# A third buffer for shuffled numerators, products 28 chunks behind the scores, and seven block products in the output projection

## Chip, cores and metric

The kernel runs on one core of one Trainium2 chip. The metric is device time in microseconds (us) of one execution. The profiled execution lists five engines: PE (TensorE: matmuls, with PEld for its weight loads), DVE (VectorE), ACT (ScalarE), POOL (GpSimd) and SP (SyncE, which here issues every DMA).

## What is computed

One layer of a diffusion backbone: RMS norm with adaLN, one input projection, two branches, one output projection. Cut to what the change touches (S = 2048 tokens, 256 context tokens, D = 1024, 4 heads, value width 128):

```python
q, k, v = _mla_qkv(u, ...)                       # latent queries
k_all = jnp.concatenate([kc, k], axis=2)         # 256 + 2048 keys
v_all = jnp.concatenate([vc, v], axis=2)
s = jnp.einsum('bhqd,bhkd->bhqk', qblk, k).astype(jnp.float32) * scale
p = jax.nn.softmax(s, axis=-1)
attn = jnp.einsum('bhqk,bhkd->bhqd', p.astype(v.dtype), v)
br_a = jax.nn.silu(gate_a) * attn
br_p = jax.nn.silu(gate_p) * _multiscale_pool(pool_in, w_pool, pool_scale)
y = jnp.concatenate([br_a, br_p], axis=-1) @ w_out[l]
x_new = x + gate[:, None, :] * y
```

Everything is float32. The kernel gets float32 accuracy out of cheaper matmuls by splitting each operand in a high part (ACT copies it to a narrower type) and a low part (the rest, by a subtraction on DVE or POOL), and makes three products: high x high, high x low, low x high.

## The kernel before

The stages are: loads and modulation (to about 100 us), the input projection and its features (`feat`, `tok`, `prod`, to about 515 us), attention (to 1124 us), output projection (to the end). The change lies in the last two.

**Attention.** There are 4 heads x 4 blocks of 512 queries. A block is two half-blocks p of 256 queries, so p runs from 0 to 31 (`NP` = 32); p is even for a block's first half and odd for its second. `scores(p, i)` (i = 0, 1: 128 queries each) makes the scores of 2304 keys in five pieces ("chunks": `CHUNKS`, four of 512 keys and one of 256), each of five matmuls (L772), the row maxima on DVE (L775), exponentials on ACT (L793) with their sums, and a 32x32 transpose on DVE (L796) into a buffer of `tbuf`. A half-block is thus ten chunks. When both i are done, `shuffle(p)` moves the 32x32 squares into place with 16 DMAs on SP (L811), from `tbuf[p % 2]` to `pbuf[p % 2]`: two shuffled buffers, both from the pool "W" (5 buffers). For the last half-block, p = 31, there is no shuffle: `pv_last` lets PE transpose.

`pv(p)` makes the products of probabilities and latent values. It has nine steps j2; for each, `halves(j2)` makes the high part on ACT (L853) and the low part on POOL (L855; on DVE for j2 = 4 and for some at the end), two steps ahead, into a tile of the pool "M" (6 buffers), and `pv_mm` makes six matmuls (L821) into the one bank "O" of a block. `norm(n)` takes a block's sums, inverts and transposes them, stores them to `rvd` (L879, L881), loads them back broadcast (`rb`, L884), loads the gate (`ga`, L886), and multiplies the two on POOL (L887). `latents(n)` splits bank O (ACT and DVE), and `finish(n)` multiplies by the value weights (three matmuls, L903) and by the gate on DVE (L905) and stores the block's branch to `brd` (L908). `finish` of a block comes at k == 2 in the products of the next.

**What sets the order.** `attn` yields after each chunk; `pv_all` is advanced so that its steps lie `LAG` = 22 chunks behind (L964: `while done < (gc - LAG) * 9 / PER`). This is the order in which the code is recorded; the framework's scheduler then sets each engine's order by simulated times, so the built order can differ. On each engine instructions run in that built order, so a waiting one holds up all behind it. `tc.issue_after(shuffle(p))` puts loads of keys (`load_k`) and of `w_out` (`load_wo`, for p in `WO_PF`) behind a shuffle on SP.

**End of attention and output.** When the scores are all recorded, about 20 steps of products remain: the last of p = 29, `pv_last` (p = 31) and `pv(30)`. Between them `out_weights` splits `w_out` in eight pieces at the steps in `WO_AT`. Then come eight pairs of 128-token tiles (t2): load of `brd` (1 MB), a split of 128x2048, and for each of 2 tiles x 2 halves of 512 columns, 8 x 3 matmuls (L1028) into a bank of "A" (5 banks); the last bank of the last pair is made in two halves of 256 columns. The result times the gate is made on DVE out of PSUM (L1049), plus x on POOL (L1052; on DVE for the last), and stored. For the first pair the matmuls are recorded by contraction steps, so that PE can start with those weights that are split first.

## Time and profile before

| | |
|---|---|
| times of 3 runs | 1288.63, 1289.4, 1295.37 us; median 1289.4 |
| profiled execution | 1288.46 us; its span (first to last instruction) 1286.7 us |
| mean granted TensorE clock | 0.984 of full speed |
| busy share: PE, PEld, DVE, ACT, POOL | 94%, 74%, 65%, 57%, 44% |
| output matmuls L1028 | 792 |
| score matmuls L772, product matmuls L821 | 1600, 1728 |

The profile's first part gives each engine's busy time; matmuls overlap, so a mean duration of one is longer than the distance between two. A row of the timeline is: start (us), duration (us), engine, line, operation, out<-in, shapes, and in brackets the idle time just before it and what ended it. A row that ends in x6 merges six instructions in a row.

### The profile page before, as it was taken

What the parts mean: (1) busy time and instruction counts of PE and PEld (TensorE: products, weight loads), DVE (VectorE), ACT (ScalarE), POOL (GpSimd) and SP (SyncE); (2) the same over time, 40 slices, a digit from 0 to 9 for tenths busy, and PEclk for the clock granted to TensorE, in tenths of its full rate; (3) what the DMA queues carried; (4) which work ended last, traced back from release to release, by engine and by line L of the source; (5) the groups of instructions that cost most, each with busy time, mean ns of one, the idle gap of its engine ahead of it and who ended that gap; (6) DMA issues with size and microseconds to landing.
All of it is one profiled execution on the core that took longest, in us unless ns stands there. A gap on an engine that the chain in (4) does not pass through costs nothing.

```text
span 1286.7 us, 22292 instructions
## 1 busy us (share of the span) xinstructions
PE 1212.8 (94%) x7805; PEld 954.5 (74%) x7805; DVE 831.1 (65%) x1595; ACT 738.5 (57%) x1780; POOL 562.1 (44%) x638
## 2 busy tenths in 40 slices
PE   6799999999999998988999989999899999899998
PEld 3698989989899998755566655666556667688887
DVE  4966654765666555677788887888778887631211
ACT  5575665655575654466777767777667777511000
POOL 3645313524344342025566645654656654332221
PEclk9799999999999999999999999999999999999999
DMA  9446952574446547367877787777777778563321
GB/s 304 149 122 138 228 137 66 130 198 136 94 108 153 113 126 196 90 150 172 199 188 181 182 203 188 182 176 196 185 176 183 179 191 236 194 238 135 115 98 49
DMA packets 208213, 208.66 MB, mean 162 GB/s; under 512 B 92339, under 2 KB 168420, under 8 KB 207974
## 3 DMA queue, kind: packets, MB, share of 16 engines
q1 hardware_dynamic: 208102, 207.25, 62.0%
q8 instruction: 61, 1.00, 0.3%
q14 instruction: 50, 0.41, 0.1%
HBM read 98.50 MB, written 35.56 MB: 104 GB/s over the span
## 4 chain that ended last, share of the span: by engine, by line
PE 70%; DMA 11%; DVE 5%; SPq 5%; ACT 4%; issue 2%; POOL 2%; ACTq 0%; DVEq 0%; POOLq 0%
PE pA L588 17%; PE pA L1028 14%; PE pA L772 14%; PE pO L821 9%; PE pA L244 6%; SPq L811 3%; PE pA L519 2%; POOL M L855 2%; DMA M<-in_w_in_dram 2%; DMA rvd<-rr 2%; ACT M L853 2%; PE pX L772 1%; DMA W<-W 1%; DVE W L796 1%; PE pA L494 1%
## 5 line engine op out<-in xcount | busy, mean ns | idle before, releaser
L855 POOL TENSOR_TENSOR M<-W,M 128x512 f16<-128x512 f32 x244 | 291.3, 1218 | 193.3 <-ACT M L853 193.2
L772 PE MATMUL pA<-B,M 128*128 128x512 f16 x1280 | 303.9, 381 | 7.0 <-ACT T L793 3.6
L588 PE MATMUL pA<-W,B 128*128 128x256 f32 x2304 | 307.3, 287 | 0.1
L588 PEld LDWEIGHTS pA<-W,B 128*128 128x128 f32 x2304 | 290.2, 192 | 3.5 <-issue 0.9
L772 PEld LDWEIGHTS <-M 128*128 128x128 f16 x1600 | 156.4, 98 | 145.6 <-issue 7.3
L821 PE MATMUL pO<-M,B 128*128 128x256 f16 x1728 | 222.1, 276 | 21.2 <-POOL M L855 20.3
L793 ACT ACTIVATE T<-pA,nm,gm 128x512 f32<-128x512 f32 x248 | 189.6, 775 | 62.7 <-DVE nm L781 62.7
L821 PEld LDWEIGHTS <-B 128*128 128x128 f16 x1728 | 168.9, 99 | 71.6 <-issue 31.6
L796 DVE STREAM_TRANSPOSE W<-T 128x512 f32<-128x512 f32 x310 | 197.6, 647 | 25.2 <-ACT T L793 14.3
L853 ACT ACTIVATE M<-W 128x512 f16<-128x512 f32 x279 | 164.7, 632 | 84.3 <-PE pO L821 65.2
L775 DVE TENSOR_REDUCE mx<-pA 128x1 f32<-128x512 f32 x256 | 173.3, 680 | 37.8 <-PE pA L772 36.3
L1028 PE MATMUL pA<-W,B 128*128 128x512 f32 (+1 forms) x792 | 178.7, 386 | 4.8 <-ACT B L96 4.8
L1028 PEld LDWEIGHTS pA<-W,B 128*128 128x128 f32 x792 | 146.0, 189 | 34.2 <-ACT B L96 5.1
L1052 POOL TENSOR_TENSOR M<-T,M 128x512 f32<-128x512 f32 x30 | 38.7, 1294 | 113.6 <-DVE T L1049 109.4
L1049 DVE TENSOR_TENSOR T<-pA,M 128x512 f32<-128x512 f32 (+1 forms) x33 | 22.0, 673 | 101.1 <-PE pA L1028 101.1
L244 PE MATMUL pA<-B,W 128*128 128x448 f32 (+1 forms) x288 | 86.4, 371 | 0.0
L97 DVE TENSOR_TENSOR B<-M,B 128x1024 fp32r<-128x1024 f32 x48 | 61.5, 1282 | 32.1 <-ACT B L96 32.0
L96 ACT ACTIVATE B<-M 128x1024 fp32r<-128x1024 f32 (+2 forms) x53 | 55.3, 1044 | 45.2 <-DMA M<-in_w_in_dram 37.5
L887 POOL TENSOR_TENSOR T<-T,T 128x512 f32<-128x512 f32 x16 | 24.6, 1540 | 82.8 <-DMA T<-gad 49.5
L96 ACT ACTIVATE B<-B 128x2048 fp32r<-128x2048 f32 x8 | 15.3, 1918 | 75.2 <-DMA B<-brd 75.2
L244 PEld LDWEIGHTS pA<-B,W 128*128 128x128 f32 x288 | 54.7, 197 | 4.4 <-DVE T L275 0.9
L244 PE MATMUL pA<-W,W 128*128 128x448 f32 (+1 forms) x144 | 52.9, 369 | 0.0
(193 smaller groups left out, 1513.4 us busy)
## 6 DMA issues: line engine op xcount, KB each, us to landing
W<-W SPq DMA_DIRECT2D x496, 144.0 KB
M<-in_w_in_dram SPq DMA_DIRECT2D x48, 512.0 KB
B<-in_x_dram SPq DMA_DIRECT2D x16, 512.0 KB
B<-brd SPq DMA_DIRECT2D x8, 1024.0 KB
M<-in_x_dram SPq DMA_DIRECT2D x16, 512.0 KB
out_dram<-M SPq DMA_DIRECT2D x15, 512.0 KB
brd<-T SPq DMA_DIRECT2D x24, 256.0 KB
kd<-T SPq DMA_DIRECT2D x36, 128.0 KB
```

Source lines behind the costliest of these rows:

```text
L96: a = nc.scalar.activation(out=hi, in_=src, func=AF.Copy)
L97: (eng or nc.vector).tensor_tensor(out=lo, in0=src, in1=hi if hi.dtype == F16 else hi.bitcast(F32), op=ALU.subtract)
L244: nc.tensor.matmul(p[:, c0:NTOK], lhsT=a[:, kt, k * 128:(k + 1) * 128], rhs=b, start=(kt == 0 and n == 0), stop=(kt == KT - 1 and n == 2))
L588: nc.tensor.matmul(p[:, i * HB:(i + 1) * HB], lhsT=w[:, a, kt, :], rhs=b[:, kt, :], start=(m == 0), stop=(m == 23))
L772: nc.tensor.matmul(b[:, s0:s0 + sn], lhsT=q[:, a, c, p % 2, i], rhs=kt[ki][:, kc, o:o + sn], start=(m == 0), stop=(m == 4))
L775: nc.vector.reduce_max(mx[:, n:n + 1], b[:, :w], axis=AX.X)
L793: nc.scalar.activation(out=e[:, :w], in_=sp[n][:, :w], func=AF.Exp, bias=ng, scale=escale, accum_out=rs[:, n:n + 1])
L796: nc.vector.transpose(TP[p][:, :, i, j0:j1, :].rearrange("p q j b -> p j q b"), e[:, :w].rearrange("p (j q b) -> p j q b", q=4, b=32))
L821: nc.tensor.matmul(o, lhsT=V[0][:, j, a], rhs=t[:, c, jj], start=(j == 0 and m == 0), stop=(j == NJ - 1 and m == 2))
L853: nc.scalar.activation(out=t[:, 0], in_=s2, func=AF.Copy)
L855: eng.tensor_tensor(out=t[:, 1], in0=s2, in1=t[:, 0], op=ALU.subtract)
L1028: nc.tensor.matmul(bank[k, n, c0][:, 0:c1 - c0], lhsT=a[:, kt, k * 128:(k + 1) * 128], rhs=w[:, c, kt % 2, n * 512 + c0:n * 512 + c1], sta ...
```

## The change

Three things are changed.

1. **Attention.** A third shuffled buffer (`pbuf[p % 3]`), which takes the last of the five "W" buffers; `LAG` is 28, and falls by a quarter chunk per chunk from chunk 280 on to 22 (`LAG_END`, `LAG_LAST`). The product of gate and inverse sums is taken out of `norm` and made by `gate_norm` just ahead of `finish`, ordered on POOL behind the last recorded low part; `finish` comes at k == 3.
2. **Output projection.** The pairs 1 to 7 are made with seven block products in place of eight. A pair's operand is 2 x 2 blocks (A00, A01, A10, A11: tile m by half k of the contraction), `w_out` is 2 x 2 blocks of 512 x 512 (B00 to B11). `sums_of` makes S1 to S4 of the A blocks on DVE, `wo_sums` makes T1 to T4 of the B blocks once, on POOL and DVE, and `out_pair` makes seven products of 4 x 3 matmuls each (`FORM`), each into its own bank, and adds them up on DVE; `close` multiplies by the gate and adds x, both on POOL (on DVE for the last block), and stores 128x512 pieces. The last product of pair 7 is made in two halves of 256 columns.
3. **First pair and weights.** Pair 0 (`plain_pair`) is still made with eight products. Its operands are split at step 16 of the remaining products. The pieces of `w_out` are now 512x512 blocks, loaded behind the shuffles of p = 26 to 29 and split at other steps; the first pair's `brd` and x are loaded behind the shuffle of p = 30; the order dependency of weights goes to the halves of `pv(30)` too.

```diff
-LAG = 22
+LAG = 28
+
+LAG_END, LAG_LAST = 28, 22
...
-WO_AT = (1, 5, 11, 12, 12, 12, 13, 13)
+WO_AT = (1, 4, 7, 10, 13, 15, 17, 18)
+BR_AT = 16
...
-        if p < 2:
+        if p < 3:
             pbuf.append(st("W", [4, 2, NJ, 32]))
-        dst = pbuf[p % 2]
+        dst = pbuf[p % 3]
...
-            nc.scalar.activation(out=t[:, 0], in_=s2, func=AF.Copy)
+            a = nc.scalar.activation(out=t[:, 0], in_=s2, func=AF.Copy)
+            if p == NP - 2:
+                tail.append(a.ins)
...
+            if eng is nc.gpsimd:
+                pool_last.append(lo.ins)
...
+    def gate_norm(ga, rb):
+
+        m = nc.gpsimd.tensor_tensor(out=ga.rearrange("p (r n) -> p r n", n=16),
...
+        order(pool_last[-1], m.ins, "the halves come first")
         return ga
...
+    def wo_sums():
...
+        b00, b01, b10, b11 = (wraw.pop((a, b)) for a in range(2) for b in range(2))
+        t1, t2 = st("B", [4, 512]), st("B", [4, 512])
+        wo_sum(t1, b01, b00, ALU.subtract, nc.gpsimd)
+        wo_sum(b01, b11, b01, ALU.subtract, nc.vector)
+        yield
+        wo_sum(t2, b01, b00, ALU.add, nc.gpsimd)
+        yield from wo_pair("T2", t2, "W")
+        wo_sum(t2, b10, t2, ALU.subtract, nc.gpsimd)
+        yield from wo_pair("T1", t1, "B")
+        yield from wo_pair("T3", b01, "B")
+        yield from wo_pair("T4", t2, "W")
...
         for k, _ in enumerate(pv_last(NP - 1)):
-            if k == 2:
-                finish(NP // 2 - 2, ol, gaus)
+            if k == 3:
+                finish(NP // 2 - 2, ol, gate_norm(*gaus))
             yield
+        gau = gate_norm(*gr_)
         yield from pv(NP - 2)
...
-    WO_PF = (28, 29, 30)
+    WO_PF = {26: (0, 0), 27: (0, 1), 28: (1, 0), 29: (1, 1)}
...
+                    lag = LAG - max(0, min(LAG - LAG_LAST, (gc - LAG_END * PER) / 4))
+                    while done < (gc - lag) * 9 / PER:
...
+    FORM = ((1, "A00", "B00"), (6, "S2", "T2"), (5, "S1", "T1"), (7, "S3", "T3"), (2, "A01", "B10"),
+            (3, "S4", "B11"), (4, "A11", "T4"))
...
+        eng = nc.vector if last else nc.gpsimd
+        for a, op in zip((g[n], xr[:, k, n]), (ALU.mult, ALU.add)):
+            if op in ops:
+                eng.tensor_tensor(out=o[:, c0:c1] if op == ALU.mult else xr[:, k, n, c0:c1], in0=o[:, c0:c1],
+                                  in1=a[:, c0:c1], op=op)
...
+        for key, a, b, op in (("S1", "A10", "A11", ALU.add), ("S2", "S1", "A00", ALU.subtract),
+                              ("S3", "A00", "A10", ALU.subtract), ("S4", "A01", "S2", ALU.subtract)):
+            v[key] = v["A10"] if key == "S3" else st("T", [4, 128])
+            nc.vector.tensor_tensor(out=v[key], in0=v[a], in1=v[b], op=op)
...
+            if i == 1:
+                p1 = st("T", [512])
+                nc.scalar.copy(out=p1, in_=pb)
+            elif i == 6:
+                u = add(pb, p1)
+            elif i == 5:
+                z = add(pb, u)
+            elif i == 7:
+                close(t2, xr, 1, 1, add(pb, z))
+                y = add(pb, u)
+            elif i == 2:
+                close(t2, xr, 0, 0, add(pb, p1))
+            elif i == 3:
+                close(t2, xr, 0, 1, add(pb, z))
+            else:
+                for c0, c1 in cols:
+                    close(t2, xr, 1, 0, add(pb, y, c0, c1), c0, c1)
```

How the built order moves, at three places. POOL in the middle of attention, before: W_6733 and W_6927 are the two shuffled buffers, L887 is the gate product of the block before.

```order
L855 TENSOR_TENSOR M_9735<-W_6733,M_9735 128x512
L855 TENSOR_TENSOR M_9751<-W_6733,M_9751 128x512
L855 TENSOR_TENSOR M_9767<-W_6733,M_9767 128x512
L855 TENSOR_TENSOR M_9783<-W_6733,M_9783 128x512
L887 TENSOR_TENSOR T_9882<-T_9882,T_9880 128x512
L855 TENSOR_TENSOR M_9885<-W_6927,M_9885 128x512
L855 TENSOR_TENSOR M_9888<-W_6927,M_9888 128x512
L855 TENSOR_TENSOR M_9891<-W_6927,M_9891 128x512
L855 TENSOR_TENSOR M_9907<-W_6927,M_9907 128x512
```

After, with the third buffer W_7083 (L860 is the low part, L898 the gate product):

```order
L860 TENSOR_TENSOR M_10073<-W_6927,M_10073 128x512
L860 TENSOR_TENSOR M_10108<-W_6927,M_10108 128x512
L860 TENSOR_TENSOR M_10163<-W_7083,M_10163 128x512
L860 TENSOR_TENSOR M_10166<-W_7083,M_10166 128x512
L860 TENSOR_TENSOR M_10169<-W_7083,M_10169 128x512
L860 TENSOR_TENSOR M_10204<-W_7083,M_10204 128x512
L860 TENSOR_TENSOR M_10253<-W_7083,M_10253 128x512
L898 TENSOR_TENSOR T_9945<-T_9945,T_9943 128x512
L860 TENSOR_TENSOR M_10277<-W_7083,M_10277 128x512
L860 TENSOR_TENSOR M_10293<-W_7083,M_10293 128x512
```

The gate product stood between the halves of an even half-block and those of the odd one behind it; it now stands behind the fifth half of a later even half-block.

POOL at the end of attention, before (W_6733 is the buffer of p = 30, L1052 the output):

```order
L855 TENSOR_TENSOR M_13563<-W_6927,M_13563 128x512
L855 TENSOR_TENSOR M_13579<-W_6927,M_13579 128x512
L887 TENSOR_TENSOR T_13464<-T_13464,T_13462 128x512
L887 TENSOR_TENSOR T_13636<-T_13636,T_13634 128x512
L855 TENSOR_TENSOR M_13778<-W_6733,M_13778 128x512
L855 TENSOR_TENSOR M_13784<-W_6733,M_13784 128x512
L855 TENSOR_TENSOR M_13835<-W_6733,M_13835 128x512
L855 TENSOR_TENSOR M_13853<-W_6733,M_13853 128x512
L1052 TENSOR_TENSOR M_13993<-T_13995,M_13993 128x512
L1052 TENSOR_TENSOR M_13993<-T_13998,M_13993 128x512
```

After (L954 is a sum of weight blocks):

```order
L860 TENSOR_TENSOR M_13569<-W_7083,M_13569 128x512
L860 TENSOR_TENSOR M_13585<-W_7083,M_13585 128x512
L898 TENSOR_TENSOR T_13471<-T_13471,T_13469 128x512
L898 TENSOR_TENSOR T_13642<-T_13642,T_13640 128x512
L860 TENSOR_TENSOR M_13788<-W_6733,M_13788 128x512
L860 TENSOR_TENSOR M_13794<-W_6733,M_13794 128x512
L860 TENSOR_TENSOR M_13835<-W_6733,M_13835 128x512
L954 TENSOR_TENSOR B_13917<-B_12701,B_12468 128x1024 x2
L860 TENSOR_TENSOR M_13855<-W_6733,M_13855 128x512
L954 TENSOR_TENSOR B_13918<-B_12701,B_12468 128x1024 x2
L954 TENSOR_TENSOR B_13918<-B_12954,B_13918 128x1024 x2
```

Both gate products still stand ahead of the halves of p = 30; a sum of two instructions now stands ahead of the last of them.

PE at the end, before: a piece in which the products of p = 30 (L821, with their weight loads) and the output matmuls of pair 0 (L1028) take turns.

```order
L1028 MATMUL pA_13914<-W_13654,B_13890 128x512
L1028 MATMUL pA_13914<-W_13654,B_13889 128x512 x2
L1028 MATMUL pA_13914<-W_13654,B_13890 128x512
L1028 MATMUL pA_13893<-W_13802,B_13889 128x512
L1028 MATMUL pA_13900<-W_13802,B_13889 128x512
L1028 MATMUL pA_13907<-W_13802,B_13889 128x512
L821 LDWEIGHTS B_6415
L821 MATMUL pO_13639<-M_13769,B_6415 128x256
L821 LDWEIGHTS B_6415
L821 MATMUL pO_13639<-M_13769,B_6415 128x256
L821 LDWEIGHTS B_6415
L821 MATMUL pO_13639<-M_13769,B_6415 128x256
```

After, the first output matmuls (L1048) and what follows them:

```order
L824 LDWEIGHTS B_6415
L824 MATMUL pO_13644<-M_13855,B_6415 128x256
L1048 MATMUL pA_13904<-W_13659,M_13864 128x512 x2
L1048 MATMUL pA_13923<-W_13659,M_13867 128x512 x2
L1048 MATMUL pA_13941<-W_13756,M_13864 128x512 x2
L1048 MATMUL pA_13956<-W_13756,M_13867 128x512 x2
L824 LDWEIGHTS B_6415
L824 MATMUL pO_13644<-M_13855,B_6415 128x256
L824 LDWEIGHTS B_6415
L824 MATMUL pO_13644<-M_13855,B_6415 128x256
L824 LDWEIGHTS B_6415
L824 MATMUL pO_13644<-M_13855,B_6415 128x256
```

Pair 0's matmuls were spread among the products of p = 30; now eight of them stand ahead of its last four matmuls, and the other 88 behind.

## Rows read from the trace of the kernel before

**Rows 1.** The page's first part: busy us, share of the span, instructions.
```profile
PE 1212.8 (94%) x7805; PEld 954.5 (74%) x7805; DVE 831.1 (65%) x1595; ACT 738.5 (57%) x1780; POOL 562.1 (44%) x638
```

**Rows 2.** Waits of PE: who waited for whom, us, times, longest us.
```profile
PE pO L821 <- POOL M L855: 20.3, 14, 4.1
PE pX L903 <- ACT T L96: 9.6, 14, 0.7
```

**Rows 3.** Stretches: length, busy us of each engine (instructions), PE clock, DMA share, GB/s.
```profile
core 0: us, PE busy (x) PEld busy (x) DVE busy (x) ACT busy (x) POOL busy (x), PEclk, DMA share, GB/s
556.00:592.00 36.00, 29.11 (x169) 16.89 (x168) 26.36 (x59) 22.97 (x55) 15.47 (x13) 0.95 0.66 155
...
758.00:768.00 10.00, 6.16 (x32) 3.63 (x31) 5.22 (x12) 6.48 (x15) 5.74 (x5) 0.83 0.95 212
...
899.00:907.00 8.00, 4.44 (x25) 2.80 (x24) 4.39 (x9) 5.00 (x13) 4.87 (x5) 0.84 1.01 236
...
937.00:945.00 8.00, 5.84 (x31) 3.36 (x30) 4.73 (x9) 5.98 (x14) 5.92 (x6) 0.81 1.02 223
...
1078.20:1099.10 20.90, 14.41 (x126) 12.42 (x123) 10.60 (x20) 13.44 (x25) 5.66 (x5) 1.00 0.82 245
1099.10:1130.00 30.90, 30.90 (x159) 24.31 (x160) 21.69 (x17) 17.23 (x20) 10.73 (x5) 0.95 0.63 208
```

**Rows 4.** Timeline: PE at 559 us; PE, POOL and SP around 760 us.
```profile
559.00 0.81 PE L821 MATMUL pO<-M,B 128*128 128x256 f16 x6 [0.85 <-POOL M L855]
...
764.95 1.44 PE L821 MATMUL pO<-M,B 128*128 128x256 f16 x6 [3.84 <-POOL M L855]
...
762.26 1.52 POOL L887 TENSOR_TENSOR T<-T,T 128x512 f32<-128x512 f32 x1 [7.90 <-DMA W<-W]
...
750.20 0.28 SPq L881 DMA_DIRECT2D rvd<-rr  x1
755.91 0.34 SPq L884 DMA_DIRECT2D T<-rvd  x1
```

**Rows 5.** Timeline of SP at 580 us, and the chain of waits at 701 us.
```profile
580.59 10.51 SPq L811 DMA_DIRECT2D W<-W  x16
...
701.47 1.98 PE pO L821 x18
```

**Rows 6.** Timeline of PE, SP and POOL at the end of attention.
```profile
1075.94 2.32 PE L772 MATMUL pA<-B,M 128*128 128x512 f16 x10
...
1124.30 5.26 PE L1028 MATMUL pA<-W,B 128*128 128x512 f32 x22
...
1097.07 0.35 SPq L884 DMA_DIRECT2D T<-rvd  x1
...
1102.88 1.66 POOL L887 TENSOR_TENSOR T<-T,T 128x512 f32<-128x512 f32 x1 [9.60 <-DMA T<-gad]
1105.80 4.10 POOL L855 TENSOR_TENSOR M<-W,M 128x512 f16<-128x512 f32 x2 [1.25 <-ACT M L853]
```

**Rows 7.** Groups by form, 1130 to 1283 us: count | busy, mean ns | idle before.
```profile
L1028 PE MATMUL pA<-W,B 128*128 128x512 f32 x648 | 147.3, 389 | 0.0
...
L1052 POOL TENSOR_TENSOR M<-T,M 128x512 f32<-128x512 f32 x30 | 38.7, 1294 | 113.6 <-DVE T L1049 109.4 <-issue 4.2
...
L1028 PE MATMUL pA<-W,B 128*128 128x256 f32 x48 | 5.9, 283 | 0.0
```

**Rows 8.** Lines (ns min/median/max, first and last start), and POOL and DVE at 1117.
```profile
L855 POOL TENSOR_TENSOR M<-W,M x244: 1139/1156/3845, 557.8 to 1120.5; 128x512 f16<-128x512 f32 x122
...
L926 DVE TENSOR_TENSOR W<-B,W x8: 1212/1223/2620, 1084.8 to 1110.9; 128x1024 fp32r<-128x1024 f32 x8
...
L97 DVE TENSOR_TENSOR T<-pO,T x16: 683/692/693, 603.0 to 1125.2; 128x512 fp32r<-128x512 f32 x16
...
1116.71 3.85 POOL L855 TENSOR_TENSOR M<-W,M 128x512 f16<-128x512 f32 x1 [6.81 <-ACT M L853]
...
1118.85 0.68 DVE L855 TENSOR_TENSOR M<-W,M 128x512 f16<-128x512 f32 x1
```

**Rows 9.** Timeline of DVE behind the last matmul.
```profile
1283.06 0.42 DVE L1049 TENSOR_TENSOR T<-pA,M 128x256 f32<-128x256 f32 x1 [2.06 <-PE pA L1028]
1283.52 0.43 DVE L1052 TENSOR_TENSOR M<-T,M 128x256 f32<-128x256 f32 x1
```

More of the change, by code (lines that the diff above doesn't have):

```diff
@@ L908, in finish @@
         nc.sync.dma_start(out=brd[0, h, :, qb * 512:(qb + 1) * 512], in_=br)
[L910 to L927 removed]
+    wo, wraw, tail = {}, {}, []
@@ L932, in pv_all @@
             if p % 2:
[L933 removed]
+                gr_ = norm(p // 2)
             for k, _ in enumerate(pv(p)):
[L935 to L936 removed]
+                if k == 3 and ol:
+                    finish(p // 2 - 1, ol, gate_norm(*gaus))
                     ol = None
```

179 lines of the change are left out of this document (109 added, 70 removed).

## The prediction, made before the result was known

> **What bounds the kernel now.** I began with the page's first part [rows 1]: TensorE (PE) is busy 94% of the span. An edit can gain here in two ways only: fewer PE cycles, or fewer gaps in PE. So I next read what PE waits for [rows 2]. One entry stands out: 20.3 us in 14 waits of the probability-value products (L821) for GpSimd's (POOL's) subtraction L855, the longest 4.1 us. The second, 9.6 us in 14 waits of at most 0.7 us, is `finish` (L903) waiting for ScalarE's (ACT's) half of `latents`; it comes once per block.
>
> The table of stretches [rows 3] shows where the gaps lie. In the short stretches at 758, 899 and 937 us PE stands still 3.8, 3.6 and 2.2 us, and the granted clock there is 0.81 to 0.84, so that each gap is paid again in slow matmuls behind it. The timeline at 760 us tells why [rows 4]: PE stops 3.84 us for POOL up to 764.95, and POOL was idle 7.90 us in front of L887, the product of gate and 1/sum in `norm`. That instruction waits for loads that SyncE (SP) could issue only from 755.91 on, because SP held still from 750.20 on until the small store `rvd` had landed. Every L855 behind L887 on POOL is late by it. So this gap is no matter of the shuffle: a late gate product blocks POOL.
>
> The last scores end at 1078.3, the first of eight output pairs at about 1129.9, 51.7 us later [rows 6]. In between SP waits for the last `rvd` until 1097.07, L887 runs at 1102.88, and only then come POOL's halves of the last numerators, the first 2 in 4.10 us. PE is idle 6.5 us of the 20.9 up to 1099.1 [rows 3] and never after that: it fills the waits with products of the first output pair. From 1130 on PE is never idle: 648 matmuls of 512 columns in 147.3 us, 0.2273 each, and 48 of 256 in 5.9 us, 0.123 each [rows 7].
>
> **The change, part by part.** All sums are made against the profiled execution: 1288.46 us, 1.8 more than its span; it lies 0.9 below the median of 1289.4.
>
> *The gate product moves* (`gate_norm`, L898, behind `pool_last`). In the order of POOL it now stands behind five halves of the next even half-block and no longer in front of an odd one's. Its loads stay where they were on SP, so they have some ten chunks more to land. That takes away the L821 waits on POOL but for the start of the first products at 559 us (0.85 [rows 4]), which stand in the order as before: 20.3 - 0.9 = 19.4 us. The slow clock behind them goes too: 36 x 0.05 + 10 x 0.17 + 8 x 0.16 + 8 x 0.19 = 6.3 us [rows 3]. What is late next is PE itself with its 0.7 us per block at L903 [rows 2]: `finish` moves to k == 3, but in the built order its first two matmuls still stand directly behind the last product of the block, so I count nothing for it (bounds: 9.6 gained, 3 lost).
>
> *Third buffer and LAG 28.* The order of PE tells what becomes of LAG: the scheduler had products of even half-blocks 26 chunks behind their scores and of odd ones 32; now it is 31 and 32 throughout, and the first product stands behind 22 chunks as before. The shuffle of an even half-block (16 DMAs, 10.51 us on SP [rows 5]) gains five chunks, and no longer waits for the products of p - 2. Alone I give this nothing, since the trace shows no L821 wait that ends with a shuffle. It is insurance, used up in the last four blocks, where the distance falls to 26, 22 and 20: there the shuffle of p = 29 stands on SP behind two loads of `w_out` and the round trip of `rvd` (5.7 us in [rows 4]), while its products stand 22 chunks behind, not 27. I add 3 us of new waits (bounds 0 and 6). Together attention: -(19.4 + 6.3) + 3 = -22.7.
>
> *The end of attention.* Two things change for the worse. On POOL both gate products of the last two blocks still stand ahead of the last numerators' halves, and ahead of the last half now stands a weight sum, two instructions of 128x1024. And the first output pair (`plain_pair`) stands behind nearly all products of p = 30 in PE's order (8 of its 96 matmuls ahead of the last four), where before it filled PE's gaps. The chain, counted from the end of the scores: gate product done at 1102.88 + 1.66 - 1078.3 = 26.2 [rows 6], if its loads land as before (the `w_out` loads are gone from in front of them, but 1 MB of x and the gate row stand there now). Then three halves at 1.16 [rows 8], two sums of about 2.6 (twice the 1.29 of a 512-wide POOL product [rows 7]), one more half: 36.0. Each shares its time with VectorE (DVE), whose weight subtractions run there without a pause; in [rows 6] two halves took 4.10 instead of 2.3. I add 4: 40.0. Behind that stand 88 matmuls x 0.2273 = 20.0, `finish` 0.7 and a slow clock of 30.9 x 0.05 = 1.5 after the gap: 62.2 against 51.7. Cost 10.5 (bounds -2 and +16).
>
> *Seven products in place of eight.* Pairs 1 to 7 took 147.3 + 5.9 = 153.2 us. Now each has 7 x 12 = 84 matmuls, one product of the last in halves of 256: 576 x 0.2273 + 24 x 0.123 = 133.9. Gain 19.3, if nothing else becomes the bound at 84 x 0.2273 = 19.1 us a pair. DVE per pair: 4 sums, 7 low parts and 7 additions at about 0.69 = 12.4 [rows 8]; POOL 8 at 1.29 = 10.3; ACT 7 splits and a copy, fewer than DVE's. All fit, side by side.
>
> The Trainium skill says in "SBUF — State Buffer", section "Who interferes with whom", that a DVE instruction with two SBUF inputs and a GpSimd instruction that reads SBUF shut each other out. The trace agrees: L855 on POOL, 1.16 us in the median, took 3.85 from 1116.71 on, while DVE ended its own L855 with two SBUF inputs at 1119.53, and stopped 1.03 us after that [rows 8]. By that rule alone the 11 two-input DVE instructions and POOL's 8 need 7.6 + 10.3 = 17.9 us of a pair one after the other, still under 19.1; the sum stays, but little is to spare.
>
> *In between and at the end.* Pair 1 needs S1 to S4, which stand on DVE behind the last evictions of pair 0: four sums and a low part, 3.4 us, against 2.7 us of the first product. With queueing 1.5 (bounds 0 and 6: the weight combinations T2 to T4, 8 low parts of 1.2 us [rows 8] and 4 more POOL sums of 2.6, must fit beside pair 0's 21.8). At the end two more 256-wide DVE instructions of 0.43 [rows 9] follow the last matmul: +0.9.
>
> Sum: -25.7 + 3 + 10.5 + 1.5 - 19.3 + 0.9 = -29.1, so 1288.5 - 29.1 = 1259.4, call it 1260.
>
> **The rivals.** *The end costs nothing.* The loads of the last gate product may land early, so that the products of p = 30 run as soon as their shuffle is there. PE then has 14.4 busy after the scores [rows 3], 54 x 0.11 = 5.9 (18 take 1.98 [rows 5]), `finish` 0.7 and 21.8 for pair 0, with the old idle time of 6.5: 49.3, a gain of 2.4. With no new waits: -25.7 - 2.4 - 19.3 + 0.9 = -46.5, 1242. For it: less data is queued ahead on SP. Against: POOL's order, which keeps the sum ahead of the last half whatever lands. Chance 0.16.
>
> *Another wait takes the place of the gate's.* The round trip of `rvd` still holds SP 5 to 7 us per block with a shuffle behind it, and `rb` now keeps its buffer a block longer, so ACT could wait for room. If only a third of the 25.7 is gained: -8.6 + 3 + 10.5 + 1.5 - 19.3 + 0.9 = -12.0, 1277. Against it: ten chunks of room. Chance 0.15.
>
> *DVE becomes the bound of the output (slower).* If each POOL instruction holds DVE up for its full length, a pair takes 12.4 + 10.3 = 22.7 on DVE. Over 7 pairs that is 25 us back: 1285. If the weight combinations run one after the other as well and pair 1 waits 10 us for T4, it is 1295, slower than before. It decides where a pair exceeds 19.1 + 29.1 / 7 = 23.3 us. For it: [rows 8]. Against: seven of DVE's 18 instructions read PSUM, and operands may be made four products ahead (M has buffers for it). The page on SBUF named above is the rule by which this would come about. Chance 0.08, half of it slower.
>
> *LAG does not do what it says*: shown above, 28 is nowhere the distance; price nothing.
>
> **How the numbers follow.** Forecast 0.61, the rivals 0.16, 0.15, 0.08. The forecast's own bounds (waits 0 to 6, end -2 to +16, start of pair 1 0 to 6) hardly all fall on one side; 1249 to 1271 holds most of it. Leaving out the far half of the rivals on either side gives 1245 to 1276. A measurement here can tell about 0.5% from no change, 6.4 us. Faster by more than that: forecast, both mild rivals: 0.92; within 0.04; slower 0.04.
>
> **What would show it right or wrong.** Right: no L821 wait for POOL in the middle blocks, PE's stretches at clock 1.00 from 600 us on; scores end near 1056; PE idle some 15 us between the scores' end and pair 0; 19.1 us a pair after. Wrong: L821 waits that end with a shuffle's DMA (LAG matters), pairs over 20 us with PE waiting for DVE (the port), or pair 0 done within 50 us of the scores' end (my price for the end is too high).

## The result, and the profile after

The changed kernel takes 1272.8 us in the median (1270.8 to 1274.5), against 1289.8 of the kernel before, run together with it: 0.9874 of its time, interval 0.9849 to 0.9899. The forecast was 1260, with a range of 1245 to 1276. The profiled execution has a span of 1270.7 us, 16.0 less than before; 29.1 were forecast.

The table splits both spans at the same four marks, read off TensorE's timeline: first score matmul, end of the last score matmul, end of output pair 0's 96th matmul, end of the last matmul. (The prediction counted 51.7 us for the third row of before; the row in [rows 6] ends at 1129.56, 51.3 behind the scores.)

| us | before | after | difference | forecast |
|---|---|---|---|---|
| up to the first score | 513.7 | 514.7 | +1.0 | 0 |
| all scores | 564.6 | 550.6 | -14.0 | -22.7 |
| scores' end to end of pair 0 | 51.3 | 64.9 | +13.6 | +10.5 |
| pairs 1 to 7 | 153.4 | 135.4 | -18.0 | -17.8 |
| behind the last matmul | 3.7 | 5.2 | +1.5 | +0.9 |

First part of the page of after (busy us, share, instructions), to hold against [rows 1]:

```profile
PE 1197.3 (94%) x7709; PEld 938.3 (74%) x7709; DVE 928.8 (73%) x1700; ACT 761.8 (60%) x1840; POOL 630.1 (50%) x672
```

PE has 96 matmuls less, DVE is busy 98 us and POOL 68 us longer. It is DVE and POOL that the rest of this document turns on. Next, the waits of PE from 600 to 1060 us of after (who waited for whom, us, times, longest):

```profile
PE pX L915 <- ACT T L99: 7.6, 11, 0.7
PE pA L775 <- ACT T L796: 3.1, 12, 0.9
PE pX L775 <- DVE rr L885: 1.4, 9, 0.2
...
PE pO L824 <- POOL M L860: 1.1, 4, 0.3
```

The same stretch of before has this for the products' waits:

```profile
PE pO L821 <- POOL M L855: 15.1, 11, 3.8
```

They are gone but for 1.1 us, and the slow stretches of [rows 3] with them: the clock is 1.00 (2.4 GHz) from 600 to 1060. But two small waits are new in every middle block, both of score matmuls: for an exponential on ACT (L796) and for `rr` (L885), DVE's copy of the transposed sums in `norm` out of the bank pX. The timelines of one middle block, without stops in either kernel, show them; of before from 866, of after from 822 us (PE rows with an idle time in front, and those just ahead of them; L876 and L883 are the transpose in `norm`):

```profile
878.77 0.74 PE L903 MATMUL pX<-T,M 128*128 128x512 f32 x2 [0.69 <-ACT T L96]
...
886.79 0.27 PE L876 MATMUL pX<-ident,s 128*4 128x128 f32 x1
886.90 1.91 PE L821 MATMUL pO<-M,B 128*128 128x256 f16 x16
888.64 1.24 PE L772 MATMUL pA<-B,M 128*128 128x512 f16 x5
889.72 0.71 PE L772 MATMUL pX<-B,M 128*128 128x256 f16 x5
```
```profile
832.04 2.35 PE L824 MATMUL pO<-M,B 128*128 128x256 f16 x20
834.58 1.24 PE L775 MATMUL pA<-B,M 128*128 128x512 f16 x5 [0.19 <-ACT T L796]
...
840.84 0.74 PE L915 MATMUL pX<-T,M 128*128 128x512 f32 x2 [0.69 <-ACT T L99]
...
850.61 0.27 PE L883 MATMUL pX<-ident,s 128*4 128x128 f32 x1
850.72 0.38 PE L824 MATMUL pO<-M,B 128*128 128x256 f16 x2
851.25 0.71 PE L775 MATMUL pX<-B,M 128*128 128x256 f16 x5 [0.15 <-DVE rr L885]
```

From its first score matmul to the next block's, an unstopped block takes 33.17 us before and 33.84 after, ten times in a row. The two new waits are the whole of these 0.67 us. A product matmul starts 0.109 us behind the one before it (18 from 848.64 to 850.61), so 20 from 832.04 on would let the score matmul start at 834.22; it starts at 834.58, 0.36 later. Behind the two from 850.72 on, the next would start at 850.94; it starts at 851.25, 0.31 later. The idle times in the brackets, 0.19 and 0.15, show half of that, since the modelled end of a matmul lies behind the start of the next. All other distances from start to start in the block are as in before, and `finish` (L903, L915) waits 0.69 us in both. The end of attention in after, PE's stops:

```profile
1086.91 7.88 PE L824 MATMUL pO<-M,B 128*128 128x256 f16 x48 [4.98 <-POOL M L860]
...
1096.36 2.18 PE L1048 MATMUL pA<-W,M 128*128 128x512 f32 x8 [1.57 <-ACT M L99]
...
1101.32 0.60 PE L824 MATMUL pO<-M,B 128*128 128x256 f16 x4 [2.78 <-POOL M L860]
...
1106.28 6.34 PE L1048 MATMUL pA<-W,M 128*128 128x512 f32 x14 [4.37 <-DVE M L100]
...
1134.30 0.73 PE L1048 MATMUL pA<-W,M 128*128 128x512 f32 x2 [1.44 <-ACT M L99]
```

What POOL and DVE did there (L898 gate product, L860 low parts, L954 weight sums, L942 weight splits, L100 operands of pair 0):

```profile
1083.08 2.22 POOL L898 TENSOR_TENSOR T<-T,T 128x512 f32<-128x512 f32 x1 [14.09 <-DMA T<-gad]
...
1093.04 6.12 POOL L954 TENSOR_TENSOR B<-B,B 128x1024 f32<-128x1024 f32 x2
1093.55 6.70 DVE L942 TENSOR_TENSOR W<-B,W 128x1024 fp32r<-128x1024 f32 x2
...
1103.40 4.03 DVE L100 TENSOR_TENSOR M<-B,M 128x512 fp32r<-128x512 f32 x3
```

The gate product is done 20 us behind the scores; in before it was 26.2 [rows 6]. Then low parts, two sums and the last low part follow as the prediction had them, but each beside DVE's weight work: two splits that take 1.21 each alone took 6.70. The last products (1101.32) then start 36.0 us behind the scores, 4 sooner than forecast; what came on top stands behind them, the 4.37 us wait for the low halves of pair 0's operands on DVE. Then the output (length, busy us by engine, clock):

```profile
core 0: us, PE busy (x) PEld busy (x) DVE busy (x) ACT busy (x) POOL busy (x), PEclk, DMA share, GB/s
1086.00:1106.30 20.30, 10.68 (x61) 7.51 (x60) 16.45 (x10) 9.39 (x14) 15.01 (x7) 0.75 0.00 0
1136.00:1264.00 128.00, 128.00 (x572) 106.23 (x571) 105.20 (x118) 29.62 (x51) 82.98 (x53) 1.00 0.41 142
```

From 1136 us on PE never waits; that part is as forecast.

### The profile page after: what moved, and what is told of

Read it like the earlier page. It is cut to its first block, busy times and chain, and to the rows that moved or that the text cites. A ratio compares the mean times of both kernels' runs of the same rounds, so it can differ in the third digit from the quotient of the medians.

```text
span 1270.7 us, 22410 instructions
## 1 busy us (share of the span) xinstructions
PE 1197.3 (94%) x7709; PEld 938.3 (74%) x7709; DVE 928.8 (73%) x1700; ACT 761.8 (60%) x1840; POOL 630.1 (50%) x672
## 4 chain that ended last, share of the span: by engine, by line
PE 71%; DMA 10%; DVE 7%; ACT 5%; SPq 3%; issue 2%; POOL 2%; DVEq 0%; ACTq 0%; POOLq 0%
PE pA L591 17%; PE pA L775 16%; PE pA L1048 12%; PE pO L824 9%; PE pA L247 6%; PE pA L522 2%; SPq L814 2%; ACT T L796 2%; PE pX L775 2%; DMA W<-W 2%; DVE W L799 1%; POOL M L860 1%; DMA M<-in_w_in_dram 1%; PE pA L497 1%; PE pX L915 1%
## 5 line engine op out<-in xcount | busy, mean ns | idle before, releaser
L860 POOL TENSOR_TENSOR M<-W,M 128x512 f16<-128x512 f32 x244 | 287.9, 1204 | 237.7 <-ACT M L856 196.4
L775 PE MATMUL pA<-B,M 128*128 128x512 f16 x1280 | 299.7, 381 | 8.4 <-ACT T L796 4.8
L591 PEld LDWEIGHTS pA<-W,B 128*128 128x128 f32 x2304 | 288.9, 191 | 3.5 <-issue 0.9
L799 DVE STREAM_TRANSPOSE W<-T 128x512 f32<-128x512 f32 x310 | 194.0, 643 | 62.7 <-ACT T L796 53.2
L824 PE MATMUL pO<-M,B 128*128 128x256 f16 x1728 | 221.4, 275 | 14.6 <-POOL M L860 10.5
L824 PEld LDWEIGHTS <-B 128*128 128x128 f16 x1728 | 169.4, 98 | 60.2 <-issue 21.5
L796 ACT ACTIVATE T<-pA,nm,gm 128x512 f32<-128x512 f32 x248 | 189.2, 773 | 9.1 <-DVE nm L784 7.7
L778 DVE TENSOR_REDUCE mx<-pA 128x1 f32<-128x512 f32 x256 | 168.3, 671 | 11.2 <-PE pA L775 10.8
L1048 PE MATMUL pA<-W,M 128*128 128x512 f32 (+1 forms) x528 | 122.9, 392 | 7.4 <-DVE M L100 4.4
L1048 PEld LDWEIGHTS pA<-W,M 128*128 128x128 f32 x528 | 99.3, 192 | 29.1 <-DVE M L100 5.0
L100 DVE TENSOR_TENSOR B<-M,B 128x1024 fp32r<-128x1024 f32 x48 | 61.6, 1285 | 33.8 <-ACT B L99 33.7
L1040 POOL TENSOR_TENSOR T<-T,M 128x512 f32<-128x512 f32 x27 | 42.4, 1573 | 46.1 <-DVE T L1088 46.1
L1040 POOL TENSOR_TENSOR B<-T,B 128x512 f32<-128x512 f32 x31 | 49.6, 1602 | 7.0 <-DVE T L1074 5.1
L1088 DVE TENSOR_TENSOR T<-pA,T 128x512 f32<-128x512 f32 (+1 forms) x50 | 33.0, 674 | 23.2 <-PE pA L1048 21.8
L796 ACT ACTIVATION_READ_ACCUMULATOR T<-pA,nm,gm 128x1 f32 x248 | 49.4, 199 | 0.0
```

The costliest lines, as they stand in the source:

```text
L100: (eng or nc.vector).tensor_tensor(out=lo, in0=src, in1=hi if hi.dtype == F16 else hi.bitcast(F32), op=ALU.subtract)
L591: nc.tensor.matmul(p[:, i * HB:(i + 1) * HB], lhsT=w[:, a, kt, :], rhs=b[:, kt, :], start=(m == 0), stop=(m == 23))
L775: nc.tensor.matmul(b[:, s0:s0 + sn], lhsT=q[:, a, c, p % 2, i], rhs=kt[ki][:, kc, o:o + sn], start=(m == 0), stop=(m == 4))
L778: nc.vector.reduce_max(mx[:, n:n + 1], b[:, :w], axis=AX.X)
L796: nc.scalar.activation(out=e[:, :w], in_=sp[n][:, :w], func=AF.Exp, bias=ng, scale=escale, accum_out=rs[:, n:n + 1])
L799: nc.vector.transpose(TP[p][:, :, i, j0:j1, :].rearrange("p q j b -> p j q b"), e[:, :w].rearrange("p (j q b) -> p j q b", q=4, b=32))
```

## Experiments

All ratios are against the kernel before, run together with each kernel. Lines in the rows shift by a few between kernels; the names in the text say what they are.

### Which part of the change gives what

**e1_gate**: the kernel before with the gate product moved, and `finish` one step later with it; buffers, `LAG` and output as in before.

```
-        nc.gpsimd.tensor_tensor(out=ga..., in1=rb..., op=ALU.mult)     # in norm
+        return ga, rb
...
-                if k == 2 and ol:
-                    finish(p // 2 - 1, ol, gaus)
+                if k == 3 and ol:
+                    finish(p // 2 - 1, ol, gate_norm(*gaus))
```

> The kernel before with one part of the change alone: the gate product (gate_norm) behind the low parts on POOL, finish at k == 3. Two buffers, LAG 22 and the old output stay; in the built order the products then stand 26 and 27 chunks behind. Theory A (the late gate product on POOL makes the attention waits): the L821 waits on POOL in the middle blocks vanish, a block takes 33.2 us, scores end 18 to 24 us earlier than 1077.9, time 1264 to 1270. Rival B (the shuffle is late, and only the third buffer with the longer distance cures it): the waits stay or move to the shuffle, since two buffers are kept; time 1284 to 1291.

Measured: 1270.8 (1270.4 to 1276.3), ratio 0.9856, interval 0.9822 to 0.9890. The products' waits for POOL from 600 to 1060 us are gone:

```profile
PE pO L821 <- POOL M L855: 0.3, 1, 0.3
```

So theory A has the cause. It also settles a doubt that [rows 4] leave open: the row of L887 names a shuffle's transfer (`W<-W`) as what ended POOL's idle time, but the shuffles and their two buffers are as before here, and the stops went with the gate product. The size is less than forecast: blocks of 33.48 (33.2), the scores end at 1063.7, 14 us earlier (18 to 24). The wait for `rr` is there, that for L793 (the exponential) is not in the middle blocks:

```profile
879.22 0.70 PE L772 MATMUL pX<-B,M 128*128 128x256 f16 x5 [0.15 <-DVE rr L880]
```

Pair 0 ends 49.0 behind the scores. This one edit gives as much as the whole change.

**e2_lag**: the kernel before with the third buffer and the larger distance alone.

```
-LAG = 22
+LAG = 28
...
-        dst = pbuf[p % 2]
+        dst = pbuf[p % 3]
```

> The kernel before with the third buffer, LAG 28 and its fall to 22 alone; the gate product stays in norm, the output stays. Products stand 31 and 32 chunks behind. Theory A: POOL still stops for the gate's load ahead of an odd half-block's low parts, so most of the 20 us of waits stay, and an undisturbed block takes 33.8 instead of 33.2 us as in the changed kernel; time 1287 to 1298. Rival B: the waits vanish, time 1265 to 1275.

Measured: 1286.8, ratio 0.9966 (0.9948 to 0.9985). Waits of PE from 600 to 1130 us:

```profile
PE pO L823 <- POOL M L857: 23.7, 41, 5.6
```

The waits of the products for POOL did not go: there are 41, all but two of at most 1.05 us, where before had few long ones (in the block at 873 us they are 0.25, 0.87 and 0.30). The gate product still stops POOL until its loads land (POOL idles 53 us in front of it from 600 to 1060 us, 55 in before). From the fourth to the fourteenth, blocks take 33.8 to 34.6, the third takes 38.4, and the scores end at 1079.3 (1078.3 before). So the distance alone spreads the waits over more and shorter ones, and pays 0.3% (0.2 to 0.5).

**e3_out**: the changed kernel with attention put back (gate product in `norm`, two buffers, LAG 22), so the new output alone.

```
-LAG = 28
+LAG = 22
...
-        dst = pbuf[p % 3]
+        dst = pbuf[p % 2]
```

> The changed kernel with the attention of before: gate product in norm, finish at k == 2, two buffers, LAG 22; the seven products, the weight sums and the new first pair stay. If the parts add up (after minus attention's 13 us of gain): pairs 1 to 7 in 134 us, scores' end to the end of pair 0 some 15 us longer than before, time 1284 to 1288. Rival C (the output part costs only since attention changed ahead of it): pair 0 ends within 55 us of the scores, time 1272 to 1278.

Measured: 1296.0, ratio 1.0043 (1.0020 to 1.0066). That is over the 1284 to 1288 at which the parts would add up. Pairs 1 to 7 take 137.8 us (135.4 in after, 153.4 in before), but the scores end at 1085.4 and pair 0 ends 66.0 behind them (before: 51.3). What PE saves in the pairs is spent at the end of attention and, 7 us of it, already in attention, where the old waits for POOL stayed (from 600 to 1130 us 20.6 us in 16 times); why they grew there was not followed up. So the new output by itself gains nothing, and the whole change no more than e1.

**e7_two**: the changed kernel with two buffers and LAG 22 (gate product and output as in after).

```
-LAG = 28
+LAG = 22
...
-        dst = pbuf[p % 3]
+        dst = pbuf[p % 2]
```

> The kernel after with the two buffers and the built distance of 26 and 27 chunks (LAG 22) in place of three buffers and 31 and 32; the gate product behind the low parts and the seven products stay. Theory A (the gate product's place is the whole gain of attention, and the longer distance lengthens each block by 0.3 to 0.4 us): blocks 33.4 to 33.5 us instead of 33.84, scores end 1060 to 1065, time 1265 to 1272. Rival B (three buffers and the longer distance carry a part of the gain): low parts and gate products come late again, blocks of 34 to 35 us, scores end at 1068 or later, time 1275 or more.

Measured: 1273.2, ratio 0.9837 (0.9788 to 0.9887), between the two forecasts; times from 1263.7 to 1279.9 where after lies within 4 us. The profiled execution was the slowest one: eight of the ten middle blocks take 33.48, but one takes 38.5 and one 36.2, each with a stop such as

```profile
772.03 0.73 PE L915 MATMUL pX<-T,M 128*128 128x512 f32 x2 [4.10 <-ACT T L99]
```

whose chain of waits leads back through the shuffle's transfers (DMA `W<-W`, 7.19 us from 757.05 on). So the buffers do what the prediction called insurance: without the third one the shuffle, with the loads queued behind it, ended last in these two blocks; in after none of the ten has such a stop, and each is 0.36 us longer.

### What holds the end of attention

**e4_lategate**: after with the last block's gate product made behind the products of p = 30.

```
-        gau = gate_norm(*gr_)
         yield from pv(NP - 2)
-        finish(NP // 2 - 1, latents(NP // 2 - 1), gau)
+        finish(NP // 2 - 1, latents(NP // 2 - 1), gate_norm(*gr_))
```

> The changed kernel with one thing moved: the last block's gate product is made after the products of p = 30 instead of before, so that POOL's last low parts don't wait for its load. Theory A: the 4.98 us stop of PE at 1086.9 goes, the products of p = 30 end 5 us earlier and pair 0 with them; time 1266 to 1270. Rival D (VectorE's and POOL's weight work, which shut each other out, sets pair 0's start, not the gate): the stop goes, but pair 0 starts within 1.5 us of before; time 1271 to 1274.

Measured: 1271.4, ratio 0.9848 (0.9815 to 0.9880): no change against after that is clear of noise, as rival D has it. The stop of 4.98 us behind the gate product is gone; others are there instead:

```profile
1094.12 1.44 PE L824 MATMUL pO<-M,B 128*128 128x256 f16 x6 [3.03 <-DVE M L860]
...
1105.86 7.90 PE L1047 MATMUL pA<-W,M 128*128 128x512 f32 x25 [6.00 <-DVE M L100]
...
1134.25 0.73 PE L1047 MATMUL pA<-W,M 128*128 128x512 f32 x2 [2.30 <-ACT M L99]
```

Pair 1's second product starts at 1134.25, in after at 1134.30. But in this profile the scores ended 3.3 us later than in that of after: the last block of scores took 42.1 us instead of 39.7, with the same number of matmuls and a granted clock of 0.92 from 1046 us to their end, 1.00 in after. Counted from the scores' end, pair 0 ends 4.7 us sooner and the last matmul 3.4 sooner. So by these profiles the edit is worth some 3 us behind the scores, and the times don't show it.

**e5_sums**: after with the weight sums ordered behind the last low part and behind pair 0's operands. Such an order sets the places in an engine's queue; it makes no engine wait for another.

```
-                order(tail[-1], i.ins, "the last block of attention comes first")
+                order(pool_last[-1], i.ins, "the last low part comes first")
+                order(first_ops[-1], i.ins, "the first pair's operands come first")
```

> The kernel after with one change at its end: the six weight-sum operations on GpSimd and the two on VectorE are ordered behind the last low part and behind the low halves of the first row pair's four operands; attention and everything else as in after. Theory D (weight work on VectorE and GpSimd that shut each other out sets when the first pair can run): the last low part is made by 1096, the wait of the last four value products on GpSimd (2.78 us) and most of the 4.37 us wait for the operands' low halves are gone, the two-operation weight split that took 6.70 us takes about 2.5, the first pair's 96th output product ends by 1119 to 1125 instead of 1130 to 1133, and the time is 1261 to 1267. Rival F (the first pair is held by the Activation queue, where the splits of the last weights stand ahead of the operands, or by the last gate product): the pair ends within 2 us of before, and the time stays 1269 to 1274. Rival H (the sums are then late for the second pair): the first pair is early by 6 or more, the second pair's second product waits by as much, and the time stays above 1268.

Measured: 1272.8, ratio 0.9851 (0.9818 to 0.9883): no change, in the range of rival F. DVE, POOL and PE (L944 weight splits, L956 sums, L1051 output matmuls):

```profile
1095.70 8.80 DVE L944 TENSOR_TENSOR W<-B,W 128x1024 fp32r<-128x1024 f32 x3
1096.75 6.67 POOL L956 TENSOR_TENSOR B<-B,B 128x1024 f32<-128x1024 f32 x2
...
1105.16 1.22 PE L1051 MATMUL pA<-W,M 128*128 128x512 f32 x2 [5.05 <-DVE M L100]
```

The last low part now came ahead of the sums, but the sums on POOL did not wait for the operands on DVE: DVE's last weight splits, in front of the operands, ran beside the sums and took 8.80 us instead of 3 x 1.21.

**e6_both**: two buffers, sums late as in e5, and the splits of the last two weight blocks behind pair 0's operands too.

```
-WO_AT = (1, 4, 7, 10, 13, 15, 17, 18)
+WO_AT = (1, 4, 7, 10, 17, 17, 18, 18)
...
+            if first_ops:
+                order(first_ops[-1], a.ins, "the first pair's operands come first")
```

> The kernel after with both: two buffers at LAG 22, the weight sums late as in the run before, and the splits of the last two weight blocks behind the first pair's operands on the Activation and Vector engines. Theory D with theory A: scores end 1061 to 1065, the first pair's 96th product ends 53 to 58 us after that, the rest takes 138 to 140 us as in after, so 1253 to 1262. Rival F: the first pair still ends 64 or more after the scores, and the time is 1265 to 1272. Rival H (late weights stop the second pair): the first pair is early but the second starts or runs over 5 us late, and the time is 1260 to 1268.

Measured: 1275.8, ratio 0.9884 (0.9851 to 0.9917): over all three times forecast for it; H had the place right (pair 1), but not the cause. Pair 0 ended at 1115.4, 52.0 behind the scores and 12.8 sooner than in after, and then PE stood still for as long:

```profile
1128.15 1.22 PE L1053 MATMUL pA<-W,M 128*128 128x512 f32 x2 [12.77 <-ACT M L99]
```

ACT waited for pair 1's source, and SP issued that load late; that it waited for a "B" buffer to come free is what e8 and e9 bear out, where one buffer more lets it go out at 1069 and 1068:

```profile
1122.20 0.37 SPq L1034 DMA_DIRECT2D B<-brd  x1
```

The same load goes out at 1122.65 in after and 1122.72 in e5.

**e8_free** and **e9_all**: the second weight sum is made in place, and pair 1's source is loaded into the buffer so saved, ahead of the sums; e8 is after with this alone, e9 is e6 with it.

```
-        t1, t2 = st("B", [4, 512]), st("B", [4, 512])
+        t1, t2 = st("B", [4, 512]), b00
...
+    br = load_br(1)
     sums = wo_sums()
```

> The kernel after with one change: the second weight sum is made in place in the buffer of the first weight block, so that one B buffer less is held, and the source of the second row pair is loaded into it ahead of the weight sums; the order of the sums, the splits and attention are as in after. Theory P (the second pair's source waits for a B buffer that the chain of weight sums frees, at 1122 to 1123 in three kernels, whatever the first pair does): the source lands before 1112, the 1.44 us wait of the second pair is gone, but the first pair still ends at 1129 to 1133, so the time falls by 0 to 3 only: 1268 to 1273. Rival D (the first pair's late start alone is the limit): nothing moves, also 1269 to 1274; the run is to be read with the next one. Rival V (the earlier load stops the write of the last blocks on the same queue): slower, 1275 or more.

> The kernel of the run that had two buffers at LAG 22, the sums late and the last weight splits behind the operands (its first pair ended 52 us after the scores, then TensorE stood 12.77 us and ran at a clock of 0.72 to 0.74), and now the second pair's source early as in the run before. Theory P: the source lands before 1110, the 12.77 us wait and the slow clock behind it are gone but for 1 to 5 us of waits for single weight products, the last matmul ends at 1250 to 1257, the time is 1255 to 1262. Rival E (the weight sums and splits themselves, which VectorE and GpSimd can only do one after the other, are the limit): the second pair starts on time and then waits 8 us or more for T1, T3 or T4; 1264 to 1272.

Measured: e8 1271.8, ratio 0.9874 (0.9850 to 0.9899); e9 1273.6, ratio 0.9885 (0.9853 to 0.9916). Both times stayed; e9's lies over both of its forecasts. In both the source is there in time, pair 0 ends early (1123.6 and 1116.5), and pair 1's second product waits again, 5.11 us in e8 and 12.96 in e9. (That pair 0 is early in e8 too was not forecast: in its built order the last low part, at 1092.22, comes ahead of the sums, from 1094.62 on.) In e9, PE and DVE (L1094 makes S1 to S4, L946 splits weights):

```profile
1132.14 1.22 PE L1060 MATMUL pA<-W,M 128*128 128x512 f32 x2 [12.96 <-ACT M L99]
...
1126.28 2.28 DVE L946 TENSOR_TENSOR W<-B,W 128x1024 fp32r<-128x1024 f32 x1
...
1129.79 1.64 DVE L1094 TENSOR_TENSOR T<-T,B 128x512 f32<-128x512 f32 x1
```

The sum S2 that the product wants stands on DVE behind all weight splits, which end at 1128.6. So the second wait was hidden behind the first.

**e10_form**: e9 with S1 to S4 of pair 1 ahead of the splits of T3 and T4, and the products in an order that wants T3 and T4 last.

```
-    FORM = ((1, "A00", "B00"), (6, "S2", "T2"), (5, "S1", "T1"), (7, "S3", "T3"), (2, "A01", "B10"),
-            (3, "S4", "B11"), (4, "A11", "T4"))
+    FORM = ((1, "A00", "B00"), (2, "A01", "B10"), (6, "S2", "T2"), (5, "S1", "T1"), (3, "S4", "B11"),
+            (7, "S3", "T3"), (4, "A11", "T4"))
...
+        if k == 4:
+            v = sums_of(br)
```

> The kernel of the last run of the step before (two buffers, sums late, operands first, second pair's source early) with two changes of order: VectorE makes the second pair's four source sums after the T1 weights and ahead of the T3 and T4 splits, and each pair runs its products in the order 1, 2, 6, 5, 3, 7, 4, so that T3 is wanted sixth and T4 seventh. Theory E (VectorE and GpSimd work on the weights one after the other until 1129 to 1132, and what TensorE waits for stood last in that queue): the 12.96 us stop at 1132 falls to under 4, the clock stays at 1.00 behind it, small waits of 1 to 3 us at products 3, 7 or 4 of the second pair; the last matmul ends at 1253 to 1258, the time is 1256 to 1263. Rival R (the queue only passes the wait on: evictions of the first pair, or T2, are now late): the sum of TensorE's waits between 1115 and 1150 stays over 9, and the time is 1268 to 1274.

Measured: 1264.5 (1262.0 to 1267.1), ratio 0.9817 (0.9785 to 0.9850). It lies between the two forecasts, and it is the first step that moves the end. Of the 12.96 us in front of the second product 3.18 are left, now for an eviction of pair 0 on DVE (L1086):

```profile
1124.30 7.14 PE L1060 MATMUL pA<-W,M 128*128 128x512 f32 x24 [3.18 <-DVE T L1086]
```

Which of the two changes of order does it, and whether they would do it without the edits of e5, e6 and e8 before them, was not run.

**e11_late**: e10 with e4's edit. **e12_three**: e11 with three buffers and LAG 28.

```
-        gau = gate_norm(*gr_)
         yield from pv(NP - 2)
-        finish(NP // 2 - 1, latents(NP // 2 - 1), gau)
+        finish(NP // 2 - 1, latents(NP // 2 - 1), gate_norm(*gr_))
```
```
-LAG = 22
+LAG = 28
...
-        dst = pbuf[p % 2]
+        dst = pbuf[p % 3]
```

> The kernel of the step before (second pair's sums ahead of T3 and T4, order 1, 2, 6, 5, 3, 7, 4; 1264.5) with one change: the last block's gate product stands behind the last half-block's low parts on GpSimd instead of ahead of them. Theory G (now that the pairs behind it start on time, the 5.29 us stop of the last half-block behind the gate product is on the path): the stop is gone, pair 0 ends 3 to 5 us sooner behind the scores, the time is 1258 to 1262. Rival E (VectorE's and GpSimd's work on the weights still ends last, so the first pair only waits longer elsewhere): the stop goes but the wait in front of the second pair grows by as much; 1263 to 1267.

> The kernel before this one in the same call, with three buffers and the built distance of 31 and 32 chunks instead of two and 26 and 27. Theory A (distance adds 0.36 us to each of the 10 to 12 middle blocks and removes the stops of 0.4 to 5 us that some blocks still have): the profile shows blocks of 33.84 with none longer, scores end within 2 us of the run with two buffers, and the medians differ by less than 4 us either way. Rival B (the third buffer is worth its place): faster by 4 us or more. Rival C (the longer distance costs): slower by 4 us or more.

Measured: e11 1258.8 (1254.7 to 1264.0), ratio 0.9764 (0.9736 to 0.9793); e12 1259.3 (1256.5 to 1261.6), ratio 0.9767 (0.9743 to 0.9792). Both lie where theory G and theory A of e12 had them. From e10 to e11 the ratio falls from 0.9817 to 0.9764, but not all of that is the edit: counted from the scores' end, the last matmul comes 3.5 us sooner than in e10, as much as the same edit gave in e4 (3.4); the scores, which stand ahead of it, ended 3.8 us earlier in this profile. Three buffers or two make no difference that these runs can tell; with three all ten middle blocks take 33.84, with two 33.48 and one of 34.3. Stretches of e11, the last one with the wait of 4.0 us in front of pair 1's second product:

```profile
core 0: us, PE busy (x) PEld busy (x) DVE busy (x) ACT busy (x) POOL busy (x), PEclk, DMA share, GB/s
...
1080.00:1096.00 16.00, 13.88 (x82) 10.89 (x80) 16.00 (x12) 12.07 (x18) 10.52 (x6) 1.00 0.15 43
1096.00:1112.00 16.00, 16.00 (x72) 13.25 (x71) 16.00 (x13) 3.04 (x4) 7.21 (x3) 1.00 0.14 38
1112.00:1128.00 16.00, 11.98 (x46) 9.41 (x45) 16.00 (x15) 7.09 (x10) 11.90 (x6) 0.89 0.28 110
```

DVE is busy all of these 48 us: what is left at the end of attention is its work. e11 and e12 are the fastest kernels here, 14 us under after. The series in one table: when pair 0 ends, when pair 1 is under way (its first matmul behind the last wait of more than 0.7 us, in front of its first or second product), and when the last matmul ends, all counted from the scores' end:

| kernel | pair 0 ends | pair 1 under way | last matmul ends | time |
|---|---|---|---|---|
| after | 64.9 | 69.0 | 200.3 | 1272.8 |
| e4_lategate | 60.2 | 65.7 | 196.9 | 1271.4 |
| e5_sums | 59.6 | 66.9 | 198.2 | 1272.8 |
| e6_both | 52.0 | 64.8 | 202.8 | 1275.8 |
| e8_free | 59.8 | 67.6 | 200.4 | 1271.8 |
| e9_all | 52.7 | 68.4 | 201.6 | 1273.6 |
| e10_form | 52.3 | 58.2 | 190.7 | 1264.5 |
| e11_late | 47.9 | 54.6 | 187.2 | 1258.8 |
| e12_three | 47.3 | 54.1 | 186.7 | 1259.3 |

The first column moves by up to 17 us; the second one stays between 64.8 and 69.0 until the last of three waits in a row (weight work in front of pair 0, buffer of pair 1's source, S2 behind the splits) is out of the way, in e10.

## Why the prediction was right, and where its terms were off

The time lies inside the range, at its far side, and the direction and the main reasons held; the gain was 17 us, not 29. What was off lies nearly all on one side: 8.7 us in the scores, 3.1 at the end of attention, 1.0 ahead of the first score, 0.6 at the very end. Point by point:

- *The gate product blocks POOL.* Right, and shown by e1. The stops that went are worth 24.2 us by the block lengths: 0.3, 4.7, 0.1 and 2.4 in the first four blocks, and 16.7 in the ten behind them (348.4 us in before, 10 x 33.17 = 331.7 without stops). 0.7 of it are 6 products that moved to later blocks. 25.7 were forecast.
- *`finish` moves, counted at nothing.* Right for `finish` itself: PE stands 0.69 us in front of it in both kernels. What the sum lacked are the two short waits of score matmuls in each middle block, 0.67 us a block and 6.7 in ten; it is the largest miss. 0.31 comes with the moved gate product (33.17 to 33.48, e1 and e7): in the new order of PE the transpose in `norm` stands two matmuls ahead of a score matmul that wants a bank of the same pool, pX; in before 21 matmuls stood between, and in e2, where blocks have no such wait, 18. That this order is the reason is read off the rows and was not tested by an edit.
- *Third buffer and LAG 28, alone worth nothing.* This term was mis-sized: with the gate product moved, they bring the other wait, for the exponential, 0.36 us a block (33.48 to 33.84, e7 against after) and 3.6 in ten. (In e2, without the moved gate product, the middle blocks have waits for POOL in its place, and the time fell by 0.3%.) As a whole the buffer costs and gives alike: e11 and e12 differ by 0.03% without and with it, and what it buys is steadiness (e7).
- *Three us for the ramp at the end.* The last two blocks took 3.5 us more, but that the number fits is luck. 24 more product matmuls stand in them (108 and 127 in before, 114 and 145 in after): 6 are missing in the first four blocks instead, and the falling distance took 18 in from behind the scores. That is 24 x 0.109 = 2.6 us of moved work. New waits, which the 3 us were meant for, make up 0.9.
- *The end of attention, +10.5.* Measured +13.6, inside the bounds, by errors that partly cancel. The chain to the last products was named rightly and took 36.0 us, not 40.0: the gate product came 6 us sooner, and from there on it was 2 slower (16.0 against 13.8, of which 4 were allowed for DVE beside POOL), since the weight work on the two engines stretched each other: in after six sums on POOL took 2.8 to 3.4 each and the splits up to 3.4 instead of 1.21. Behind the last products 28.8 us passed, not 22.2: the wait of 4.37 us for the low halves of pair 0's operands, which stand on DVE behind the weight splits, is in no term of the sum, and the clock was 0.75 from 1086 to 1106 us where 1.5 us were allowed. That the gate product sets the end (36.0 of the 40.0 were counted from it) is half true: with it out of the way (e4) pair 0 ended 4.7 us sooner behind the scores, and then DVE, busy without a pause from 1086 to 1106 us, held it with waits of 3.03 and 6.00 us.
- *Pair 1, +1.5.* The wait was 1.44 in front of its second product, and pairs 1 to 7 came out at 135.4 as forecast (133.9 + 1.5). But what was "queueing" in the text is a chain of three waits, each hidden behind the one before it, and it is why e5, e6, e8 and e9 did not move the time.
- *Seven products, -19.3.* Right. The rival that DVE and POOL bound the output fell: in 128 us PE was busy for 128, DVE for 105.2, POOL for 83.0.
- *Behind the last matmul, +0.9.* Measured +1.5.
- The sign to look for, "scores end near 1056", was wrong (1065.3): 6.7 from the blocks, 1.5 from stops, 0.5 from the ramp, 1.0 from a later start. The others held: no wait of products for POOL in the middle blocks to speak of, the clock at 1.00, 16.1 us of idle PE from the scores' end to 1106 (15 forecast), and pairs of 19.0 us (19.1).

The rival "another wait takes the place of the gate's" has the time nearest to the result, but it did not happen as told: waits for `rvd` or for room are in no row of PE's waits in attention, and 24.2 of the 25.7 us came, not a third. Waits did take a part of the gain back, but two others, and 6.7 us of it.

## What to carry to other kernels

When an edit takes a stop away, measure the stretch between stops too, and from start to start: two waits that the profile shows with 0.15 and 0.19 us cost 0.31 and 0.36, and 0.67 us a block ate a quarter of the gain. Before you compare two kernels by a mark such as the scores' end, count the work on each side of it: here 18 product matmuls, 2 us, had moved across. When several queues drain at a seam between two stages, single edits that give nothing are no proof that their wait was harmless; take the waits away together, in the order in which the traces bring them up. Work that is moved from TensorE to the other engines (18 us saved here) is paid where those engines are already full, not where it is used (e3).
